# Last block of a hybrid SSD/GLA trunk: gate projections of the next-to-last head moved behind the last head's values, u in one tile per 128 features, operands of the first products split inside the block

## The chip, the core and the metric

The kernel runs on one core of one Trainium2 chip. The metric is the device time of one execution in microseconds (us). TensorE (PE) does the matmuls, VectorE (DVE) and ScalarE (ACT) the elementwise work, GpSimd (POOL) a smaller share of it, and SyncE (SP) issues most DMAs. PE and SP run in the order in which the program issues; ACT, DVE and POOL get their order from a scheduler at build time, and each then works through its own list in that order.

## What is computed

One layer of a decoder trunk on 2048 tokens (16 meta tokens ahead of them) with 1024 features, all in float32:

```python
u = rmsnorm(hres, norm_w)
proj = jnp.einsum('bld,dn->bln', u, w_in)
z, xbc, dt_raw, q, k, v, g_gla, a_lr, merge_g = split_cols(proj, IN_WIDTHS)
# y_ssd: 4 groups of a chunked state-space scan;  o: 4 heads of chunked gated linear attention (GLA)
y_gla = o.reshape(b, l, GLA_DV) * jax.nn.silu(g_gla)
branch_proj = jnp.einsum('blnc,ncd->blnd', branches, w_branch)
gates = jax.nn.sigmoid(merge_g.reshape(b, l, N_BRANCH, D_MODEL))
merged = jnp.sum(gates * branch_proj, axis=2)
return hres + jnp.einsum('bld,de->ble', merged, w_out)      # and a last rmsnorm
```

## The kernel before

**Precision.** Each float32 operand of a large matmul is split into a high part (ACT, cast to float32r) and a low part (DVE, the rest); helper `split` (L232) does the pair. `accum` (L183) then issues three matmuls per product, high by high (L185), high by low (L186) and low by high (L187). So a "projection" of 128 output features over 512 tokens is 8 x 3 = 24 matmuls of 512 columns (`proj_feat`).

**First part: four blocks of 512 tokens.** For each block `load_u` makes the normalized input u, high and low, for 8 groups of 128 features (index kt), into one tile of a pool of two (`upool`), and writes u to DRAM too (`u_left`). Then come four SSD groups (`ssd_proj`) and four GLA heads (`gla_proj`). `gla_proj` of head h projects q, k, the values v (`proj_tok`, two halves), then two gate tiles g, and starts that head's scan. A scan (`gla_scan`) is a generator with about ten steps; each `yield` of a projection runs one step of every scan that is under way, so a scan's small matmuls stand between the big projections in PE's list. The steps of a GLA scan, with their lines: score products of six levels (`level_in` L698 to L705 on DVE and ACT, `level_out` L713 on PE, merged by L717 and L720), sums for the diagonal (L783), merge and masks (L785, L788, L791), transposes of the keys (`turn_keys`, L734) and of the attention tile (L800), two state updates (`advance`: matmuls L185 to L187, DVE L809), outputs of two chunks each (L821 and L185 to L187 on PE, copy and squares L825, L828 on ACT), then the normalization (L228 DVE, L229 POOL, L832 ACT), transposes (L837) and the product with the gate (L838 DVE). In the last block the scan of the last head (3) starts right behind its values, ahead of its gates; all other heads' scans start behind their gates.

**Second part: seven matrix products** in stages (merge gates, two branches, output), each computed with seven block products p = 1..7 instead of eight per pair of tiles (`Stage`). A product is 12 matmuls of 512 columns. Its left operand comes from weight tiles (`load_a` L931, sums on POOL L940 to L943, split `prep_a` L949/L950), its right operand from u, y or the merged values in DRAM (`load_b` L919, split `prep_b` L924/L925), 4 pieces for each p. The first stage's products p = 1 and 2 take u of block 0 as right operand; p = 6 and 7 take sums that were stored earlier.

**The seam.** When the last projection is issued, the remaining scan steps run in a loop; a table `between` says what of the second part is issued ahead of each step. Before the change: loads and splits of the operands of p = 1 and p = 2, and the products p = 1 and p = 2 of the first two tile pairs (n = 0, 1) (`NEARLY = 4`). The pools of the second part lie on memory of the first: `u`, the weight tiles (`wpool`), and later the scans' tiles. A tile there can be filled only once the last reader of what lay there is done. The pools of the later operands (`bops6`, `outs`) open only behind the last scan step.

Of the kernel before, what the change touches and what calls it, by code (L numbers as in the profile page):

```python
# [14 lines left out]
P = 128  # L15
D = 1024
# [12 lines left out]
NC1 = 8  # L29
LEVELS = (64, 32, 16, 8, 4, 2)  # L30
# [10 lines left out]
def trunk_kernel(ctx: ExitStack, tc: tile.TileContext, xm, xmt, w_feat, w_tok, w_zm, w_br, w_o,  # L41
# [71 lines left out]

    inputs = ctx.enter_context(ExitStack())
    upool = inputs.enter_context(tc.tile_pool(name="upool", bufs=2))
# [85 lines left out]
    def proj_tok(key, src, u, starts, banks, width=256, per=2, sub=None):  # L201

        nq = KT // per
        opened = set()
        for q0 in range(0, nq, 2):
            if q0 == nq // 2:
                yield
            ws = [load_w(f"{key}_{q}", src[:, q * per * width:(q + 1) * per * width]) for q in (q0, q0 + 1)]  # L210
            for i, ((bk, ps), a) in enumerate(zip(banks, starts)):
                c0 = sub if sub is not None and i >= NCH else 0
                for k2 in range(2 * per):
                    kt = q0 * per + k2
                    h, lo = ws[k2 // per]
                    cs = slice(k2 % per * width + c0, (k2 % per + 1) * width)
                    accum(ps[:, c0:width], tuple(t[:, kt, a:a + P] for t in u),
                          (h[:, cs], lo[:, cs]), bk not in opened, kt == KT - 1, skip_group_check=True)
                    opened.add(bk)
# [16 lines left out]

    def load_u(b):
# [3 lines left out]
        pair = mk(upool, [P, 2, KT * (META + BLK)], F32R, "u")[:, :, :KT * tt]  # L241
        uh, ul = [pair[:, i].rearrange("p (k t) -> p k t", k=KT) for i in range(2)]

        def rows_load(r0, n, i=None):
            xt = mk(wk, [P, D], F32, "tok4", bufs=NT4) if i is None else mk(wk, [P, META + BLK], F32, "acc")[:, :BLK]
            nc.sync.dma_start(xt[:n], xm[r0:r0 + n, :] if i is None else xm[r0:r0 + n, i * BLK:(i + 1) * BLK])
            return xt
# [44 lines left out]
        if m0:  # L292
            rm = bank(pt, "pt")
            nc.tensor.matmul(rm[:, :META], rs[NCH][:META].to_broadcast([META, P]), ident[:META, :META],
                             start=True, stop=True)
            rbs = [(rm, 0, META)] + rbs
        else:
            rbc = mk(wk, [P, 3 + META + BLK], F32, "cin")[:, :BLK]
            nc.scalar.activation(rbc, rb, AF.Copy)
            rbs = [(rbc, 0, BLK)]  # L300
            yield
        for kt in range(KT):
            xk = mk(wk, [P, META + BLK], F32, "act" if m0 else "acc", bufs=NACT if m0 else 2)[:, :tt]
# [4 lines left out]
            nc.scalar.activation(uh[:, kt, :tt], xk, AF.Copy)  # L308
            nc.scalar.dma_start(u_left[b][kt], xk[:, m0:])
            nc.vector.tensor_tensor(ul[:, kt, :tt], xk, uh[:, kt, :tt].bitcast(F32), op=ALU.subtract)  # L310
            yield
        return uh, ul
# [42 lines left out]
    def new_block(b, u):  # L355
        o = Block()
        o.b, o.u = b, u
        o.m0 = META if b == 0 else 0
        o.tt = o.m0 + BLK
        o.segs_all = [(0, o.tt // 2), (o.tt // 2, o.tt // 2)] if b == 0 else [(0, BLK)]  # L360
        o.segs_real = [(o.m0, BLK)]
        o.starts = [o.m0 + c * P for c in range(NCH)]
        o.chunks = ([(0, META)] if o.m0 else []) + [(a, P) for a in o.starts]
        o.ci0 = 1 if o.m0 else 0
        o.nck = len(o.chunks)
        for nm in ("tkd", "tkc", "wde", "ecu", "dec"):
            setattr(o, nm, mk(bpool, [P, 5, NH], F32, nm, bufs=2))
# [3 lines left out]
        o.mov = lambda kt, a, n: tuple(t[:, kt, a:a + n] for t in u)  # L371
        return o


    def dt_chain(o, psd):
# [44 lines left out]
        cr = mk(wk, [P, 3 + META + BLK], F32, "cin")[:NH, :BLK]  # L420
# [39 lines left out]
    def ssd_proj(o, g):  # L460
# [16 lines left out]
        for j in range(4):  # L477
            ti = g * 4 + j
            pss = proj_feat(f"s{ti}", w_feat[T_SSD + ti], o.segs_all, o.mov)
            cin = mk(wk, [P, 3 + META + BLK], F32, "cin")  # L480
            acc = mk(wk, [P, META + BLK], F32, "acc")[:, :tt]
# [18 lines left out]
    def fetch_cb(o, g, c):  # L500
        cbs[g, c] = cb = mk(wk, [P, 4, P], F32, "cb", bufs=3)
# [113 lines left out]
    def gla_proj(o, h):  # L615
# [27 lines left out]
        yield  # L643
        for j in range(2):
# [6 lines left out]
        if not last:  # L651
            begin(gla_scan(o, h, qs, kf, (vh, vl), vm, gs))
# [208 lines left out]

    ordered = ExitStack()
    ordered.enter_context(tc.manual_schedule(engines={mybir.EngineType.PE, mybir.EngineType.SP}))
    for b in range(nblk):
        o = new_block(b, next_u[b])
        for i in range(SG + GH):
# [4 lines left out]
            if i == SG and b + 1 < nblk:  # L871
                begin(fetch_u(b + 1))
# [21 lines left out]
    bpl = {p: pool2(f"bops{p}", 4) for p in (1, 2)}  # L894
    rpl = pool2("raws", 1)
    apl = pool2("aops", 6)
    bt_raws = {"early": (rpl, "br0", 2)}
# [6 lines left out]
    class Stage:  # L904
# [16 lines left out]
        def prep_b(self, p, j):  # L921
            raw = self.braws[p, j]
            t = mk(bpl[p], [P, 2, BLK], F32R, f"b{p}")
# [13 lines left out]
        def sum_a(self, n):  # L937
            a11, a21, a22, a12 = self.araws.pop(n)
            s1, s2, s4 = [mk(rpl, [P, 4, P], F32, "as", bufs=6) for _ in range(3)]
# [13 lines left out]
        def product(self, n, p, early=False):  # L953
# [10 lines left out]
            if p in (1, 6, 5):  # L964
                sn = mk(rpl, [P, 4, P], F32, "as", bufs=6).rearrange("p k c -> p (k c)") if early else mk(opl, [P, BLK], F32, "sn", bufs=6)
                nc.scalar.activation(sn, ps, AF.Copy)  # L966
                self.snap[n, p] = sn
# [3 lines left out]


# [106 lines left out]
    NEARLY = 4  # L1079
    order[:NEARLY] = [(stages[0], n, p) for n in range(2) for p in (1, 2)]  # L1080
# [14 lines left out]
    for si, st in enumerate(stages):  # L1095
        for q in range(0 if si else 8, 28):
            p, j = PS[q // 4], q % 4
            pos = begins[si] - 12 + 0.8 * q if si else -0.99 + 0.2 * (q // 4) if q < 16 else 2 * (q // 4 - 4)
# [29 lines left out]
    st = stages[0]  # L1128

    def b_ops(p, js):  # L1130
        for j in js:
            st.load_b(p, j)
            st.prep_b(p, j)
# [20 lines left out]
    bpl.update({p: pool2(f"bops{p}", 4, side="right") for p in (6, 7, 5, 3, 4)})  # L1154
    opl, spl = pool2("outs", 1, side="right"), pool2("small", 4, side="right")
    bt_raws["all"] = opl, "br", 5

    with tc.manual_schedule(engines={mybir.EngineType.SP}):
        run(-1)
        for i, (st, n, p) in enumerate(order):  # L1160
            if i >= 2:
# [92 lines left out]
```

## Time and profile before

| | us |
|---|---|
| median of 3 runs | 2304.4 (2302.48 to 2305.96) |
| profiled execution, its own time | 2306.7 |
| its span, first to last instruction | 2304.9 |
| PE busy in the span | 2236.0 |
| DVE, ACT, POOL busy | 1546.8, 1181.4, 677.5 |
| mean granted TensorE clock | 0.989 |

The profile has a page (busy time per engine, 40 slices, the chain that ended last, the costliest groups of instructions, DMA issues), and the trace behind it answers views: stretches of time (windows) with each engine's busy time and the granted clock, waits (who waited for whom), the timeline of single instructions, and groups of instructions by line. A row of a group reads: line, engine, operation, tile written <- tiles read, shape, count | busy us, mean ns of one | idle time ahead of it and what ended it. Matmul ends are modelled and consecutive matmuls overlap, so the pace of a row of matmuls is read from start to start.

### The profile page before, as it was taken

The page shows a single profiled execution, that of the slowest core. Times are in us where ns is not written, and L with a number is a line of the kernel's source. Part 1 is how long each engine was busy: PE and PEld are TensorE (multiplying, and loading weights), DVE is VectorE, ACT ScalarE, POOL GpSimd, SP SyncE. Part 2 cuts the span into 40 slices and gives each one's busy share as a digit, 9 for nine tenths or more (in the row PEclk, how much of TensorE's full clock was granted, in tenths as well). Part 3 has the DMA queues.
Part 4 walks back from the last instruction along what each step waited for, and adds up shares of the span by engine and source line. Part 5 has one row for each costly group of instructions (what it writes and reads, how often), then busy time and mean ns, then how long its engine had stood idle before and what let it go on. Part 6 is the DMA issues. An engine that isn't in the chain of part 4 may idle for free.

```text
span 2304.9 us, 36458 instructions
## 1 busy us (share of the span) xinstructions
PE 2236.0 (97%) x12641; PEld 1954.7 (85%) x12641; DVE 1546.8 (67%) x2895; ACT 1181.4 (51%) x2726; POOL 677.5 (29%) x681
## 2 busy tenths in 40 slices
PE   7899999999999999999999999889999999999998
PEld 6899989888889888888888888778878888788786
DVE  5677676676666676666667555754588945788766
ACT  4665654465544465544455534554554545454443
POOL 3344433122222122321212100136333274324331
PEclk9999999999999999999999999999999999999999
DMA  8756776667787666887676654466677865778743
GB/s 299 236 202 221 268 262 206 220 197 241 247 263 230 210 223 216 259 262 235 200 233 209 213 159 156 138 218 207 219 246 275 312 220 204 235 268 266 245 152 121
DMA packets 301544, 518.04 MB, mean 225 GB/s; under 512 B 27696, under 2 KB 143664, under 8 KB 301360
## 3 DMA queue, kind: packets, MB, share of 16 engines
q1 hardware_dynamic: 200400, 402.84, 53.8%
q10 hardware_dynamic: 100960, 112.88, 14.0%
q8 instruction: 99, 1.62, 0.3%
q14 instruction: 85, 0.70, 0.1%
HBM read 368.42 MB, written 147.19 MB: 224 GB/s over the span
## 4 chain that ended last, share of the span: by engine, by line
PE 78%; DMA 7%; DVE 6%; ACT 4%; issue 3%; POOL 1%; SPq 0%; ACTq 0%; DVEq 0%; POOLq 0%
PE pj L185 18%; PE pj L187 18%; PE pj L186 18%; PE pt L185 3%; PE pt L187 3%; PE pt L186 3%; PE pc L574 2%; PE pc L185 2%; PE pc L186 2%; PE pc L187 2%; PE pc L713 2%; DMA br<-out_t 1%; PE pc L575 1%; PE pc L577 1%; DMA acc<-in_xmt 1%
## 5 line engine op out<-in xcount | busy, mean ns | idle before, releaser
L185 PE MATMUL pj<-u,whl 128*128 128x512 f32 (+1 forms) x1184 | 445.9, 377 | 12.3 <-ACT acc L485 6.3
L187 PE MATMUL pj<-u,whl 128*128 128x512 f32 (+1 forms) x1184 | 431.8, 365 | 0.5 <-DVE tkc L392 0.5
L186 PE MATMUL pj<-u,whl 128*128 128x512 f32 (+1 forms) x1184 | 430.9, 364 | 0.0
L185 PE MATMUL pj<-whl,u 128*128 128x256 f32 (+1 forms) x992 | 287.8, 290 | 1.8 <-ACT u L308 1.5
L187 PE MATMUL pj<-whl,u 128*128 128x256 f32 (+1 forms) x992 | 282.4, 285 | 1.5 <-DVE u L310 1.5
L186 PE MATMUL pj<-whl,u 128*128 128x256 f32 (+1 forms) x992 | 282.1, 284 | 0.0
L185 PEld LDWEIGHTS pj<-u,whl 128*128 128x128 f32 x1184 | 225.9, 191 | 50.2 <-ACT acc L485 7.6
L185 PE MATMUL pj<-b,a 128*128 128x512 f32 x640 | 254.1, 398 | 14.1 <-ACT sn L966 8.2
L187 PEld LDWEIGHTS pj<-u,whl 128*128 128x128 f32 x1184 | 225.4, 190 | 36.6 <-POOL whl L166 0.8
L186 PEld LDWEIGHTS pj<-u,whl 128*128 128x128 f32 x1184 | 226.0, 191 | 33.1
L187 PE MATMUL pj<-b,a 128*128 128x512 f32 x640 | 252.9, 395 | 0.0
L186 PE MATMUL pj<-b,a 128*128 128x512 f32 x640 | 251.7, 393 | 0.0
L80 POOL TENSOR_TENSOR wr<-wr 128x256 f32<-128x256 f32 x80 | 67.1, 839 | 432.2 <-DMA wr<-u 177.0
L185 PEld LDWEIGHTS pj<-whl,u 128*128 128x128 f32 x992 | 189.7, 191 | 3.1 <-ACT u L308 1.8
L187 PEld LDWEIGHTS pj<-whl,u 128*128 128x128 f32 x992 | 189.7, 191 | 2.2 <-DVE u L310 2.2
L186 PEld LDWEIGHTS pj<-whl,u 128*128 128x128 f32 x992 | 189.9, 191 | 0.3
L925 DVE TENSOR_TENSOR b<-br,b 128x512 fp32r<-128x512 f32 x196 | 154.8, 810 | 50.3 <-ACT b L924 49.6
L166 POOL TENSOR_TENSOR whl<-wr,whl 128x512 fp32r<-128x512 f32 (+1 forms) x100 | 133.9, 1346 | 179.8 <-ACT whl L165 127.2
L940 POOL TENSOR_TENSOR as<-ar,ar 128x512 f32<-128x512 f32 x40 | 58.2, 1455 | 417.7 <-DMA ar<-in_w_br 201.7
L489 DVE SCALAR_TENSOR_TENSOR acc<-cin,hcw,acc 128x512 f32<-128x512 f32 (+1 forms) x192 | 154.8, 806 | 27.1 <-ACT acc L485 26.2
L924 ACT ACTIVATE b<-br 128x512 fp32r<-128x512 f32 x196 | 119.2, 626 | 102.7 <-DMA br<-br_t 40.4
L950 DVE TENSOR_TENSOR a<-ar,a 128x512 fp32r<-128x512 f32 x160 | 126.8, 801 | 60.6 <-ACT a L949 59.8
(278 smaller groups left out, 5057.2 us busy)
## 6 DMA issues: line engine op xcount, KB each, us to landing
whl<-k_s SPq DMA_DIRECT2D x96, 512.0 KB, 4.3
whl<-k_g SPq DMA_DIRECT2D x96, 512.0 KB, 4.2
whl<-k_v SPq DMA_DIRECT2D x48, 512.0 KB, 3.7
whl<-k_z SPq DMA_DIRECT2D x36, 512.0 KB, 3.7
wr<-in_w_feat SPq DMA_DIRECT2D x64, 256.0 KB, 4.4
k_s<-whl SPq DMA_DIRECT2D x32, 512.0 KB, 3.6
cb<-cumd ACTq DMA_DIRECT2D x64, 256.0 KB, 5.7
y<-gg ACTq DMA_DIRECT2D x64, 256.0 KB, 4.5
```

Source lines behind the costliest of these rows:

```text
L80: nc.gpsimd.tensor_tensor(o, x, y, op=ALU.subtract)
L166: nc.gpsimd.tensor_tensor(hl[:, 1], raw, hl[:, 0].bitcast(F32), op=ALU.subtract)
L185: nc.tensor.matmul(ps, sh, mh, start=first, stop=False, **kw)
L186: nc.tensor.matmul(ps, sh, ml, start=False, stop=False, **kw)
L187: nc.tensor.matmul(ps, sl, mh, start=False, stop=last, **kw)
L489: nc.vector.scalar_tensor_tensor(acc, cin[:, k:k + tt], hcw[:, ti, k:k + 1], acc, op0=ALU.mult, op1=ALU.add)
L574: nc.tensor.matmul(py[:, h * 64:(h + 1) * 64], dm[:, h], xdt[:, h], start=True, stop=True)
L713: nc.tensor.matmul(ps[:, r * P:(r + 1) * P], kq[:, 2 * r * P:(2 * r + 1) * P], kq[:, (2 * r + 1) * P:(2 * r + 2) * P], start=True, stop=True)
L924: nc.scalar.activation(t[:, 0], raw, AF.Copy)
L925: nc.vector.tensor_tensor(t[:, 1], raw, t[:, 0].bitcast(F32), op=ALU.subtract)
L940: nc.gpsimd.tensor_tensor(s1, a21, a22, op=ALU.add)
L950: nc.vector.tensor_tensor(t[:, 1], src, t[:, 0].bitcast(F32), op=ALU.subtract)
```

## The change

Four edits go together.

- **Order.** In the last block the scans of heads 2 and 3 (`LATE_G = 2`) both start behind their own values. The two gate projections of head 2 are put aside (`late_g`) and issued behind head 3's values, ahead of head 3's own two.
- **u in tiles.** u lives in 8 tiles per block, one per 128 features: even blocks in pool `ueven`, which stays open to the end, odd blocks in `uodd`.
- **Operands of p = 1, 2.** A generator `first_b`, begun with head 0 of the last block, loads u of block 0 back from DRAM, one 128-feature tile a step, through the buffers of raw weights (`wr`), and splits it into `ueven` tiles, which the last block doesn't use.
- **The seam.** `between` is rewritten: it issues the loads of the left operands, p = 1 and 2, and now p = 6 too for n = 0, 1 (`NEARLY = 6`), with the four right operands of p = 6 loaded through one raw buffer (`br0`, 1 instead of 2). Some small tiles move to a pool (`spool`) that lies between `ueven` and `uodd`; `bops6` opens on its memory.

The diff, cut to its core:

```diff
+    ueven = ctx.enter_context(tc.tile_pool(name="ueven", bufs=KT))
-    upool = inputs.enter_context(tc.tile_pool(name="upool", bufs=2))
+    spool = inputs.enter_context(tc.tile_pool(name="spool", bufs=2))
+    uodd = inputs.enter_context(tc.tile_pool(name="uodd", bufs=KT))
...
+    def u_tile(b):
+        return mk(uodd, [P, 2, BLK], F32R, "uo") if b % 2 else mk(ueven, [P, 2, META + BLK], F32R, "ue")
...
-        last, gs = (o.b, h) == (nblk - 1, GH - 1), []
+        last, gs = o.b == nblk - 1 and h >= LATE_G, []
         if last:
-            begin(gla_scan(o, h, qs, kf, (vh, vl), vm, gs, True))
+            begin(gla_scan(o, h, qs, kf, (vh, vl), vm, gs, h == GH - 1))
...
+        if last and h < GH - 1:
+            late_g.append(gla_gates(o, h, gs))
+            return
+        for gen in late_g:
+            yield from gen
+        late_g.clear()
+        yield from gla_gates(o, h, gs)
+        if not last:
+            begin(gla_scan(o, h, qs, kf, (vh, vl), vm, gs))
...
+    def first_b():
+        loaded = []
+        for n in range(KT + 1):
+            if n < KT:
+                raw = mk(wpool, [P, 512], F32, "wr", bufs=NWR)
+                nc.sync.dma_start(raw, u_left[0][n])
+                loaded.append(raw)
+            if n:
+                t = u_tile(0)[:, :, :BLK]
+                split(t[:, 0], t[:, 1], loaded[n - 1])
+                early_b[1 + (n - 1) // 4, (n - 1) % 4] = t
+            yield
...
-            if i == SG and b + 1 < nblk:
-                begin(fetch_u(b + 1))
+            if i == SG:
+                begin(fetch_u(b + 1) if b + 1 < nblk else first_b())
...
-    bt_raws = {"early": (rpl, "br0", 2)}
+    bt_raws = {"early": (rpl, "br0", 1)}
...
     between = {
-        0: [lambda: st.load_a(0), lambda: b_ops(1, (0, 1))],
-        1: [lambda: b_ops(1, (2, 3)), lambda: st.prep_a(0, 1)],
-        2: [lambda: st.load_a(1), lambda: b_ops(2, (0, 1))],
-        3: [lambda: b_ops(2, (2, 3)), lambda: st.prep_a(0, 2)],
-        4: [lambda: st.product(0, 1, True), lambda: st.prep_a(1, 1)],
-        5: [lambda: st.sum_a(0)],
-        6: [lambda: st.product(0, 2), lambda: st.prep_a(1, 2)],
-        7: [lambda: st.sum_a(1)],
+        0: [lambda: st.load_a(0), lambda: st.load_a(1), lambda: st.load_b(6, 0)],
+        1: [],
+        2: [lambda: st.prep_a(0, 1), lambda: st.prep_a(1, 1)],
+        3: [lambda: early(0, 1), lambda: st.prep_a(0, 2)],
+        4: [lambda: st.sum_a(0), lambda: early(1, 1), lambda: st.prep_a(1, 2)],
+        5: [lambda: early(0, 2), lambda: st.prep_b(6, 0), lambda: st.load_b(6, 1)],
+        6: [lambda: early(1, 2), lambda: st.sum_a(1), lambda: st.prep_b(6, 1), lambda: st.load_b(6, 2)],
+        7: [lambda: st.prep_a(0, 6), lambda: st.prep_b(6, 2), lambda: st.load_b(6, 3)],
+        8: [lambda: st.prep_b(6, 3), lambda: early(0, 6), lambda: st.prep_a(1, 6)],
+        9: [lambda: early(1, 6)],
     }
```

More of the change, by code (lines that the diff above doesn't have):

```diff
@@ L210, in proj_tok @@
             ws = [load_w(f"{key}_{q}", src[:, q * per * width:(q + 1) * per * width]) for q in (q0, q0 + 1)]
-            for i, ((bk, ps), a) in enumerate(zip(banks, starts)):
-                c0 = sub if sub is not None and i >= NCH else 0
+            for n, ((bk, ps), a) in enumerate(zip(banks, starts)):
+                c0 = sub if sub is not None and n >= NCH else 0
                 for k2 in range(2 * per):
@@ L370, in new_block @@
         o.alr = mk(bpool, [P, 5, 48], F32, "alr")
[L371 removed]
+        o.mov = lambda kt, a, n: tuple(u[kt][:, i, a:a + n] for i in range(2))
         return o
@@ L964, in product @@
             if p in (1, 6, 5):
-                sn = mk(rpl, [P, 4, P], F32, "as", bufs=6).rearrange("p k c -> p (k c)") if early else mk(opl, [P, BLK], F32, "sn", bufs=6)
-                nc.scalar.activation(sn, ps, AF.Copy)
-                self.snap[n, p] = sn
+                if early and p == 6:
+                    return
+                self.snapshot(n, p, early)
             if p in DONE:
@@ L1078, in trunk_kernel @@
             order += [(st, n + i, p) for p in ps for i in range(2)]
-    NEARLY = 4
-    order[:NEARLY] = [(stages[0], n, p) for n in range(2) for p in (1, 2)]
+    NEARLY = 6
     AHEAD, LOAD = 5, 9
@@ L1153, in trunk_kernel @@
     first.close()
-    bpl.update({p: pool2(f"bops{p}", 4, side="right") for p in (6, 7, 5, 3, 4)})
+    bpl.update({p: pool2(f"bops{p}", 4, side="right") for p in (7, 5, 3, 4)})
     opl, spl = pool2("outs", 1, side="right"), pool2("small", 4, side="right")
     bt_raws["all"] = opl, "br", 5
+    for n in range(2):
+        st.snapshot(n, 6)
     with tc.manual_schedule(engines={mybir.EngineType.SP}):
```

65 lines of the change are left out of this document (39 added, 26 removed).

## The prediction

> **What bounds the kernel now.** I read the page first, then stretches of time, then PE's timeline where a stretch isn't full. The page's head and busy line:
>
> ```profile
> span 2304.9 us, 36458 instructions
> PE 2236.0 (97%) x12641; PEld 1954.7 (85%) x12641; DVE 1546.8 (67%) x2895; ACT 1181.4 (51%) x2726; POOL 677.5 (29%) x681
> ```
>
> PE is the bound. The change removes no matmul: set side by side, the two builds issue the same 11,908 PE instructions, 2897 on DVE, 2979 on ACT. So only PE's idle time and lost clock can change. The stretches around the seam (columns: PE, PEld, DVE, ACT, POOL busy, then PEclk):
>
> ```profile
> 1300.00:1415.00 115.00, 115.00 (x723) 103.96 (x722) 58.98 (x147) 48.93 (x127) 7.17 (x9) 1.00 0.51 159
> 1415.00:1460.00 45.00, 45.00 (x281) 40.54 (x280) 26.12 (x64) 18.29 (x49) 1.58 (x1) 1.00 0.53 169
> 1460.00:1480.00 20.00, 16.17 (x88) 13.59 (x86) 16.12 (x41) 8.56 (x21) 0.00 (x0) 1.00 0.34 118
> 1480.00:1500.00 20.00, 13.14 (x61) 11.62 (x62) 17.48 (x37) 11.49 (x29) 8.93 (x6) 0.74 0.43 137
> 1500.00:1520.00 20.00, 14.15 (x70) 11.86 (x69) 8.04 (x14) 11.12 (x27) 4.77 (x4) 0.96 0.33 115
> 1520.00:1545.00 25.00, 23.87 (x92) 18.77 (x92) 17.98 (x28) 17.91 (x32) 3.10 (x3) 0.89 0.86 289
> 1545.00:1645.00 100.00, 100.00 (x439) 82.09 (x438) 48.89 (x62) 46.91 (x82) 58.67 (x55) 1.00 0.67 220
> ```
>
> PE is full on both sides and loses time from 1472 to 1541 only. Every idle piece there, from PE's timeline (the bracket holds the idle time and what ended it):
>
> ```profile
> 1474.31 0.71 PE L713 MATMUL pc<-sq 128*128 128x128 f32 x4 [1.39 <-DVE c L720]
> 1476.15 0.70 PE L821 MATMUL pc<-s_gla,act 128*128 128x256 f32 x2 [1.13 <-DVE c L809]
> 1481.50 1.22 PE L713 MATMUL pc<-sq 128*128 128x128 f32 x4 [2.81 <-ACT junk L828]
> 1483.25 1.23 PE L713 MATMUL pc<-sq 128*128 128x128 f32 x4 [0.53 <-DVE c L720]
> 1493.46 0.41 PE L800 MATMUL pt<-cst,sq 128*128 128x128 f32 x2 [4.17 <-DVE sq L791]
> 1499.33 0.38 PE L185 MATMUL pc<-tok,kdt 128*128 128x256 f32 x1 [0.66 <-DVE c L809]
> 1519.50 1.22 PE L185 MATMUL pj<-b,a 128*128 128x512 f32 x2 [5.85 <-ACT b L924]
> 1540.30 0.51 PE L185 MATMUL pj<-b,a 128*128 128x512 f32 x1 [1.13 <-ACT sn L966]
> ```
>
> Their sum is 17.7 us. After three of them the clock stands at half for a while:
>
> ```profile
> 1480.90:1487.70 6.80, 5.67 (x20) 4.97 (x21) 6.32 (x17) 3.72 (x10) 0.00 (x0) 0.50 0.75 252
> 1494.60:1498.00 3.40, 3.40 (x16) 3.13 (x14) 3.40 (x5) 0.91 (x3) 3.40 (x3) 0.51 0.03 8
> 1518.50:1525.30 6.80, 5.80 (x14) 4.50 (x15) 3.97 (x6) 4.51 (x8) 0.00 (x0) 0.50 0.87 291
> ```
>
> Half of the 5.67 + 3.40 + 5.80 busy us is lost: 7.4. **The seam costs 17.7 + 7.4 = 25.1 us**, the ceiling of what this change can bring. What PE waits for: to 1500, head 3's scan, with head 2's in the same DVE list and only two gate projections as filler; at 1519.5, the right operands of p = 6, whose loads wait for the scan's last transposes.
>
> **Part 1, the order: about 11 us more filler.** One projection's length, from its first matmul to what follows it:
>
> ```profile
> 1458.77 0.47 PE L185 MATMUL pj<-u,whl 128*128 128x512 f32 x1
> 1464.33 0.60 PE L713 MATMUL pc<-sq 128*128 128x128 f32 x4
> 1465.47 0.61 PE L713 MATMUL pc<-sq 128*128 128x128 f32 x4
> ```
>
> 5.56 us; two are 11.1. Behind head 3's values now stand four, 22.2 us, and by the new order about 10 us of the scans' own matmuls: 32 us in which head 3's scan can reach its last level product. Does it? Before, values ended about 1457 and that product came at 1487.4, 30 us, of which DVE was busy 33.6 of the 40 us to 1500 with both scans and eight low parts of b. Now those eight are gone from here, and head 2's scan is 11 us further ahead, since it waits for values only. Adding such rows' durations along the new DVE list, each piece no earlier than the matmul it waits for, I find head 3's work ahead of the last level product done some 4 us before PE gets there. The tightest place is head 3's first level product: before, 8.4 us after the values (1465.47, no idle time); now 9.1. So PE stays full to the end of the fourth projection, and the 1.39, 1.13, 2.81 and 0.53 go. Cost if this cover fails: up to those 5.9 us.
>
> **Then the chain is bare.** Behind the fourth projection the new PE list has the last level product and the sums (1.14 us from start to start, 1464.33 to 1465.47), head 2's transposes and the key transposes (about 1.3): 2.45 us. The attention transposes (L800) wait meanwhile for this DVE list, with the same operations' rows from before:
>
> ```profile
> L785 DVE COPY_PREDICATED c<-msk,pt 128x256 f32<-128x256 uint8 x2 | 0.9, 435 | 0.0
> L788 DVE TENSOR_TENSOR sq<-c,cst 128x512 f32<-128x512 f32 x2 | 1.4, 688 | 0.0
> L791 DVE COPY_PREDICATED sq<-msk,pt 128x512 f32<-128x512 uint8 x2 | 1.4, 724 | 0.0
> L648 DVE SCALAR_TENSOR_TENSOR gg<-gg,pj 128x512 f32<-128x512 f32 x2 | 1.4, 678 | 0.0
> L838 DVE SCALAR_TENSOR_TENSOR gg<-pt,hgw,gg 128x512 f32<-128x512 f32 x4 | 3.0, 744 | 2.0 <-PE pt L837 2.0
> L950 DVE TENSOR_TENSOR a<-ar,a 128x512 fp32r<-128x512 f32 x4 | 2.8, 689 | 1.9 <-ACT a L949 1.9
> L647 ACT ACTIVATE gg<-pj 128x512 f32<-128x512 f32 x2 | 1.2, 591 | 2.5 <-PE pj L187 2.5
> ```
>
> In its order: tanh of the last gate (0.59), L648 0.68, L785 0.44, L838 0.74, L788 0.69, L838 0.74, L950 0.69, L791 0.72: 5.3, less some 0.07 overlap for each of seven, with 0.2 for the hand-overs: 5.0. **PE idles 5.0 - 2.45 = 2.5 us** (4.17 before).
>
> Behind it no product stands between state updates and outputs any more: before, p = 1 stood there (22 matmuls from 1500.13 to 1505.14 in the timeline); now both p = 1 products come after the last outputs. So PE sees: the attention's low parts behind two low parts of a, two L950 (0.7); state updates (0.3); and, ahead of the last outputs, the copy and squares of the first, whose bank they take:
>
> ```profile
> 1500.40 0.60 ACT L825 ACTIVATE ot<-pc 128x512 f32<-128x512 f32 x1 [4.64 <-PE pc L187]
> 1501.67 0.19 ACT L828 ACTIVATION_READ_ACCUMULATOR junk<-pc 128x1 f32 x1
> ```
>
> 1.46 us, 0.4 of it beside the state matmuls: 1.1. **Sum 2.1 us**; between nothing (all hidden) and 4.9, if it is as uncovered as two chains of 2.45.
>
> **Part 2, clock.** Does 2.5 us of idle time halve the clock?
>
> ```profile
> 1999.90 0.79 PE L185 MATMUL pj<-b,a 128*128 128x512 f32 x1 [2.12 <-ACT sn L966]
> 1999.80:2003.10 3.30, 3.20 (x8) 2.53 (x9) 2.39 (x4) 2.61 (x6) 0.00 (x0) 0.50 0.19 70
> ```
>
> 2.12 us did, for 3.3 us; 1.13 at 1540.30 came into a full-speed stretch. I take one such window over a tail that is partly waiting anyway: **1.5 us** (ends: 0 and, for a 6.8 us window, 3.4). The Trainium skill (TensorE: Matmul & The Clock Gate, section "What's actually happening") has the clock fall after at least one idle window of about 3.4 us; by that rule 2.5 us would cost no clock, and the sum would be 1.5 us lower. The 2.12 us row speaks against it.
>
> **Part 3, operands of p = 1, 2, 6.** Rows of before for a split and for the normalization (cast, low part, POOL's power, ACT's scaling):
>
> ```profile
> L924 ACT ACTIVATE b<-br 128x512 fp32r<-128x512 f32 x11 | 6.4, 620 | 1.3 <-DMA br<-u 1.3
> L925 DVE TENSOR_TENSOR b<-br,b 128x512 fp32r<-128x512 f32 x8 | 5.8, 741 | 1.0 <-ACT b L924 1.0
> L229 POOL TENSOR_TENSOR rstd<-rstd,mhalf 128x4 f32<-128x4 f32 x2 | 2.4, 1196 | 50.1 <-DVE rstd L228 50.1
> L832 ACT ACTIVATE ot<-ot,rstd 128x256 f32<-128x256 f32 x12 | 5.1, 496 | 1.1 <-POOL rstd L229 1.1
> ```
>
> Eight loads, eight casts (0.62 each) and eight low parts (0.74) move from the seam into heads 0 and 1 of the last block: there DVE is busy 59 of 115 us and ACT 49, so 5.9 and 5.0 more are hidden by PE's 115 of 115; uncovered they would cost that. On SP they stand between weight loads; PE's waits from 1290 to 1472 are none, so those loads have room. The p = 6 operands now load on memory that is free early, so **the 5.85 us go, and their 2.9 of clock**. But they come one at a time through one buffer, and ACT's list has the second piece's cast ahead of the copy of the last outputs. A 256 KB load alone, and in a crowd:
>
> ```profile
> 1490.90 2.75 DMA br<-u
> 1515.01 5.87 DMA br<-gate_t
> ```
>
> That load starts when the first piece's low part is done, about when the second state update is. The normalization behind it is 1.46 (copy, squares), 1.2 on POOL, four scalings that take 5.1 / 12 = 0.43 each; the two p = 1 products that hide all this last 24 x 0.233 = 5.6. With 2.75 the transposes L837 wait 0, with 5.87 about 1.9: **0.9 us**. The other three pieces have 18 us (p = 1, transposes, p = 2 and part of p = 6) for three rounds of load and split, 2.75 to 5.87 plus 1.36 each; I take nothing, 4 at the far end. What is late next, p = 7, loads after the transposes with 11 us of p = 2 and 6 as cover: nothing. The 1.13 at a snapshot (L966) stays: **1.1**.
>
> **Part 4, u in tiles.** Blocks 0 to 3 up to head 0 of the last block keep order and waits on every engine, and so does the time after the first stage. The first left operands can load once the last projection has read its first feature tiles, not all of u; as the product that needs them comes over 12 us later, that is worth nothing here.
>
> **The sum.** Left at the seam: 2.5 + 2.1 + 1.5 + 0.9 + 1.1 = 8.1 us, of 25.1. Gain 17.0. The profiled span 2304.9 becomes 2287.9 (its own time, 2306.7, 2289.7); the runs' median is 2304.4, 0.5 below the span: **2287.4**.
>
> **Rivals.**
> - *The clock stays full* (the Trainium skill's rule above) and the load is fast: 8.1 - 1.5 - 0.9 leaves 5.7, gain 19.4, 2285.0. For it: at 1540.30 nothing happened; against it: 2.12 us was enough elsewhere.
> - *ACT's list holds the tail*: the second piece lands late (5.87), the last outputs' copy waits, the transposes with it, and the idle time halves the clock again: 1.9 - 0.9 + 3.4 + some late p = 6, gain 12 to 13, 2292.
> - *The waiting moves on*: the scan's chain is as slow as before (4.17 again, 4.9 between the states, both at half clock) and p = 6 waits its 4 us. Left: 4.2 + 4.9 + 3.4 + 4 = 16.5 with the snapshot's; gain 8.6, 2296. Against it: before, DVE had two low parts of b in the 4.6 us from the sums to L800, and the clock was just back from half.
> - *Nothing*: first-stage operands arrive no earlier, PE reaches them sooner and waits: within 5 us of now. Against it: in 1520 to 1545 PE was held 1.1 us while 20 pieces came.
> - *Slower*: place, SP's list in heads 0 and 1. A raw load waits for its buffer until the split three loads back is done; weight loads stand behind it. If each of eight were held past the weights' lead, one projection's 5.6 us or so, and by 3 us more, PE would lose 8 x 3 = 24 against 17 gained: 2311. It decides from 2.1 us a piece. Against it: the split awaited is three projections, 16 us, old, and blocks 1 and 2 carry more such loads with no idle time.
>
> **How the numbers follow.** Forecast 2287.4: 0.47. Full clock 2285.0: 0.15. ACT held 2292: 0.15. Moves on 2296: 0.11. Nothing: 0.05. Slower: 0.07. Range 2283 to 2296: from the ceiling less 4 us of left idle time to the fourth case, which it holds half. 0.2% is 4.6 us, about what a measurement here can tell from none. Faster (under 2299.8) 0.88, same 0.05, slower 0.07.
>
> **What would show it.** In PE's waits of the new profile: at the seam no L713 row, no L924 row of 5.8; an L800 row of about 2.5; rows of 1 or less at L185 and L821; an L837 row up to 2. Half clock in one window. A wait for `whl` in heads 0 and 1 would be the slower case; a wait for b6 of over 3 us would break part 3; idle time ahead of the fourth gate projection's end, part 1.

## The result: 11.8 us faster, 6 us short of the forecast

The changed kernel takes **2293.55 us** (median of five runs, 2291.95 to 2295.66); the kernel before, in runs beside it, 2305.37 (2302.48 to 2306.14). The ratio is 0.9951, 95% interval 0.9937 to 0.9966: faster by half a per cent, clear of the noise, and 6.1 us above the 2287.4 of the forecast. The profiled span fell by 12.9 us, from 2304.9 to 2292.0, where 17.0 was forecast. Head and busy line of the page after:

```profile
span 2292.0 us, 36448 instructions
PE 2232.7 (97%) x12641; PEld 1944.7 (85%) x12641; DVE 1549.2 (68%) x2895; ACT 1180.1 (51%) x2726; POOL 683.8 (30%) x681
```

The counts of matmuls and of DVE's and ACT's instructions are those of before, PE is 3.3 us less busy, and the rest of the gain is idle time. Lines have moved: L800 is now L819 (attention transposes), L713 L732 (level products), L828 L847 (squares), L821 L840 (outputs), L837/L838 L856/L857 (output transposes, gate products), L924/L925 L958/L959 and L949/L950 L983/L984 (splits of b and a), L966 L1010 (snapshot: the copy of a product's PSUM bank to SBUF, ahead of the next product that adds to the bank), L940 to L943 L974 to L977 (POOL's sums). The same stretches as before (busy time of PE, PEld, DVE, ACT, POOL, then PEclk):

```profile
1300.00:1415.00 115.00, 115.00 (x727) 104.23 (x727) 66.69 (x160) 54.56 (x140) 7.24 (x9) 1.00 0.55 176
1415.00:1460.00 45.00, 43.28 (x272) 38.78 (x271) 32.06 (x84) 19.86 (x54) 1.01 (x1) 1.00 0.44 145
1460.00:1480.00 20.00, 18.08 (x100) 15.48 (x99) 10.86 (x29) 8.42 (x23) 1.01 (x1) 1.00 0.27 91
1480.00:1500.00 20.00, 15.76 (x85) 12.52 (x84) 11.01 (x21) 9.89 (x25) 2.27 (x2) 1.00 0.50 159
1500.00:1520.00 20.00, 19.08 (x84) 14.43 (x83) 16.58 (x19) 12.13 (x23) 15.01 (x10) 1.00 0.75 235
1520.00:1545.00 25.00, 23.62 (x99) 18.29 (x99) 19.78 (x23) 13.65 (x25) 17.24 (x16) 1.00 0.80 258
1545.00:1645.00 100.00, 100.00 (x437) 81.75 (x436) 51.45 (x66) 49.22 (x86) 50.07 (x45) 1.00 0.64 212
```

The clock column is full in every row (0.74, 0.96 and 0.89 before), and 1480 to 1500 has 15.8 us of PE instead of 13.1. But 1415 to 1460, full before, now lacks 1.7 us, and 1500 to 1545 still lacks 2.3. PE's pieces with idle time ahead of them (in brackets), of 0.3 us or more:

```profile
1429.82 0.71 PE L732 MATMUL pc<-sq 128*128 128x128 f32 x4 [0.54 <-DVE c L739]
1439.76 1.16 PE L732 MATMUL pc<-sq 128*128 128x128 f32 x8 [1.19 <-ACT junk L847]
...
1466.26 1.16 PE L732 MATMUL pc<-sq 128*128 128x128 f32 x8 [1.39 <-ACT junk L847]
1475.45 0.71 PE L732 MATMUL pc<-sq 128*128 128x128 f32 x4 [0.53 <-DVE c L739]
1483.53 0.66 PE L856 MATMUL pt<-cst,ot 128*128 128x128 f32 x4 [0.33 <-DVE c L804]
1486.76 0.41 PE L819 MATMUL pt<-cst,sq 128*128 128x128 f32 x2 [1.93 <-DVE sq L810]
1488.77 0.39 PE L189 MATMUL pc<-tok,atp 128*128 128x256 f32 x1 [0.36 <-ACT atp L237]
1489.62 0.38 PE L191 MATMUL pc<-tok,atp 128*128 128x256 f32 x1 [0.34 <-DVE atp L238]
1490.34 0.70 PE L840 MATMUL pc<-c,act 128*128 128x256 f32 x2 [0.34 <-DVE c L828]
1493.05 0.70 PE L840 MATMUL pc<-c,act 128*128 128x256 f32 x2 [0.95 <-ACT junk L847]
...
1519.36 0.74 PE L189 MATMUL pj<-b,a 128*128 128x512 f32 x2 [0.78 <-ACT b L958]
1520.76 0.51 PE L190 MATMUL pj<-b,a 128*128 128x512 f32 x1 [0.66 <-DVE b L959]
1526.91 0.50 PE L189 MATMUL pj<-b,a 128*128 128x512 f32 x1 [0.51 <-ACT sn L1010]
```

With pieces under 0.3 us the sum is 10.2 us, against 17.7. The 5.85 ahead of p = 6 is gone and the 4.17 at the attention transposes is 1.93, as forecast. What was not forecast: 3.65 us at level products while projections still run (first four rows; the first two are head 2's level products, in front of and between the halves of head 3's values, the other two head 3's, between gate projections), and the waits of p = 5 at 1519 and 1520.

**A measure that noise spares.** Executions of one kernel differ by several us in places far from the seam: in the profiles of this case one group of waits in the first 160 us (L492) takes from 5.3 to 8.1 us, those at the snapshots behind 2000 us from 3.8 to 7.3. So I compare the profiles by one stretch of PE's own list, from the last state product ahead of the last block's head 2 (1384.8 after) to a matmul of the first stage behind all that differs (1582.4 after), cut at the last head's sums and at its last output. us:

| kernel | to the sums | sums to last output | from there on | whole stretch |
|---|---|---|---|---|
| before | 102.0 | 18.7 (one product p = 1 of 5.1 within) | 88.5 | 209.2 |
| changed | 97.0 | 12.8 | 87.8 | 197.6 |
| changed, second profile | 97.1 | 12.4 | 87.5 | 196.9 |

11.6 of the 12.9 us arise here. What follows uses the times for the verdicts and this stretch for the parts.

### The profile page after: what moved, and what is told of

Read it like the earlier page. It is cut to its first block, busy times and chain, and to the rows that moved or that the text cites. A ratio compares the mean times of both kernels' runs of the same rounds, so it can differ in the third digit from the quotient of the medians.

```text
span 2292.0 us, 36448 instructions
## 1 busy us (share of the span) xinstructions
PE 2232.7 (97%) x12641; PEld 1944.7 (85%) x12641; DVE 1549.2 (68%) x2895; ACT 1180.1 (51%) x2726; POOL 683.8 (30%) x681
## 5 line engine op out<-in xcount | busy, mean ns | idle before, releaser
L189 PE MATMUL pj<-ue,whl 128*128 128x264 f32 (+1 forms) x672 | 238.8, 355 | 12.3 <-ACT acc L492 6.3
L191 PE MATMUL pj<-ue,whl 128*128 128x264 f32 (+1 forms) x672 | 232.3, 346 | 0.6 <-DVE tkc L399 0.6
L190 PE MATMUL pj<-ue,whl 128*128 128x264 f32 (+1 forms) x672 | 231.3, 344 | 0.0
L189 PE MATMUL pj<-uo,whl 128*128 128x512 f32 x512 | 206.6, 404 | 0.0
L191 PE MATMUL pj<-uo,whl 128*128 128x512 f32 x512 | 200.1, 391 | 0.0
L190 PE MATMUL pj<-uo,whl 128*128 128x512 f32 x512 | 199.4, 389 | 0.0
L189 PE MATMUL pj<-b,a 128*128 128x512 f32 x480 | 189.4, 396 | 6.6 <-ACT sn L1010 5.8
L191 PE MATMUL pj<-b,a 128*128 128x512 f32 x480 | 188.6, 393 | 0.0
L190 PE MATMUL pj<-b,a 128*128 128x512 f32 x480 | 187.8, 391 | 0.7 <-DVE b L959 0.7
L974 POOL TENSOR_TENSOR as<-ar,ar 128x512 f32<-128x512 f32 x40 | 59.1, 1476 | 396.3 <-DMA ar<-in_w_br 114.2
L984 DVE TENSOR_TENSOR a<-ar,a 128x512 fp32r<-128x512 f32 x160 | 125.5, 793 | 57.0 <-ACT a L983 55.3
L959 DVE TENSOR_TENSOR b<-br,b 128x512 fp32r<-128x512 f32 x140 | 120.5, 877 | 52.6 <-ACT b L958 50.7
L189 PEld LDWEIGHTS pj<-ue,whl 128*128 128x128 f32 x672 | 128.9, 192 | 29.9 <-ACT acc L492 7.4
L189 PE MATMUL pj<-whl,ue 128*128 128x256 f32 (+1 forms) x496 | 144.1, 291 | 2.1 <-ACT ue L315 2.1
L189 PE MATMUL pj<-whl,uo 128*128 128x256 f32 (+1 forms) x496 | 143.3, 289 | 0.6 <-DMA whl<-k_zm 0.6
L191 PEld LDWEIGHTS pj<-ue,whl 128*128 128x128 f32 x672 | 128.9, 192 | 15.8 <-POOL whl L170 0.9
L191 PE MATMUL pj<-whl,ue 128*128 128x256 f32 (+1 forms) x496 | 140.6, 284 | 1.4 <-DVE ue L317 1.4
L190 PEld LDWEIGHTS pj<-ue,whl 128*128 128x128 f32 x672 | 129.1, 192 | 14.8
L191 PE MATMUL pj<-whl,uo 128*128 128x256 f32 (+1 forms) x496 | 140.8, 284 | 0.0
```

What stands on the lines that cost most here:

```text
L189: nc.tensor.matmul(ps, sh, mh, start=first, stop=False, **kw)
L190: nc.tensor.matmul(ps, sh, ml, start=False, stop=False, **kw)
L191: nc.tensor.matmul(ps, sl, mh, start=False, stop=last, **kw)
L959: nc.vector.tensor_tensor(t[:, 1], raw, t[:, 0].bitcast(F32), op=ALU.subtract)
L974: nc.gpsimd.tensor_tensor(s1, a21, a22, op=ALU.add)
L984: nc.vector.tensor_tensor(t[:, 1], src, t[:, 0].bitcast(F32), op=ALU.subtract)
```

## Experiments

**Each part alone.** The kernel before with only the gates' order changed:

```diff
-        last, gs = (o.b, h) == (nblk - 1, GH - 1), []
+        last, gs = o.b == nblk - 1 and h >= LATE_G, []
...
+        if last and h < GH - 1:
+            late_g.append(gla_gates(o, h, gs))
+            return
```

> The kernel before with the order of the last block's gates alone: head 2's two gate projections run behind head 3's values; operands of the first stage, u and pools as before. Theory A (both parts earn, each at its own place): the idle time up to the attention transposes falls from 13.2 us (1.39, 1.13, 2.81, 0.53, 4.17, 0.66 and 2.5 between) to 6 or so, the 5.85 us wait for the right operands of p = 6 stays and halves the clock behind it: gain 3 to 6 us, 2299 to 2302. Rival B (the gain is the operands' alone): gain under 1 us, about 2304.5. Rival C (all of it is the order): gain 10 or more, 2295 or less.

Measured: 2300.19 us, ratio to before 0.9978 (0.9967 to 0.9988); stretch 206.1, so 3.1 less than before: theory A's size. Up to the last head's sums it takes 97.1, as in the changed kernel. The rest is spoilt; three of its waits and a stretch:

```profile
1492.71 0.41 PE L813 MATMUL pt<-cst,sq 128*128 128x128 f32 x2 [1.93 <-DVE sq L804]
...
1519.42 0.73 PE L186 MATMUL pj<-b,a 128*128 128x512 f32 x2 [0.92 <-ACT b L937]
1522.40 0.79 PE L187 MATMUL pj<-b,a 128*128 128x512 f32 x1 [2.25 <-DVE b L938]
```

```profile
1500.00:1520.00 20.00, 17.98 (x75) 14.46 (x73) 12.40 (x17) 12.37 (x30) 11.70 (x9) 0.81 0.59 191
```

The attention transposes wait the same 1.93 as in the changed kernel (4.17 before), so the order alone is enough for that gain. p = 6 still waits, 3.2 us and not the 5.85 that theory A kept: its loads still begin only behind the last output transposes (1513.06), but PE reaches it 5.4 us after that, with two products p = 2 in between. And the clock is lost: 0.81 over these 20 us.

The changed kernel with the order of before:

```diff
-LATE_G = 2
+LATE_G = 3
```

> The changed kernel with LATE_G = 3: operands, u and pools as changed, the last block's projections in the order of before (head 2's gates ahead of its scan and of head 3). Theory A: the 5.85 us wait and its half clock go (8.7 us), the new waits at p = 7 and p = 5 (1.7 us and some slower matmuls) come; the 1.39, 1.13, 2.81, 0.53 and 4.17 ahead of the transposes stay within 1 us: gain 6 to 8, 2297 to 2299. Rival B (operands alone earn everything): gain 11 to 12, 2293 to 2294. Rival C (all of it is the order): gain under 2.

Measured: 2296.99 us, ratio 0.9970 (0.9959 to 0.9982); stretch 202.0, 7.2 less than before: theory A again. With 3.1 that makes 10.3 of 11.6; neither part earns it all. One point of theory A fails: the 4.17 ahead of the attention transposes doesn't stay, 1.20 is left there and 1.77 at the sums in front. What the old order leaves at the seam:

```profile
1474.43 0.71 PE L732 MATMUL pc<-sq 128*128 128x128 f32 x4 [1.37 <-DVE c L739]
1476.28 1.22 PE L840 MATMUL pc<-s_gla,act 128*128 128x256 f32 x2 [1.13 <-DVE c L828]
1482.07 1.16 PE L732 MATMUL pc<-sq 128*128 128x128 f32 x8 [1.73 <-ACT junk L847]
```

**u in tiles alone**: the kernel before with the new pools and `u_tile`, nothing else.

```diff
-        pair = mk(upool, [P, 2, KT * (META + BLK)], F32R, "u")[:, :, :KT * tt]
+        u = []
...
+            u.append(u_tile(b)[:, :, :tt])
```

> The kernel before with u in tiles per 128 features, two pools of them, and nothing else of the change. Prediction's step (u in tiles is worth nothing by itself): within 1 us of before in the stretch from 1384 to 1582, within 0.2% in time. Rival (blocks gain because a tile of u comes free before the block's last projection): faster by 2 us or more, in the blocks ahead of the seam.

Measured: 2301.69 us beside 2303.02 for before, ratio 0.9993 (0.9984 to 1.0003): nothing, as forecast. Its stretch is 206.7, 2.5 shorter, missing the 1 us I gave it; 1.8 of that is clock, 0.83 against 0.74 in the 20 us from 1480.

**Why level products wait (3.65 us).** The releaser of the two longest waits is the last of ACT's squares (L847), which read the PSUM bank; pool `pc` has two. Edit, on all heads:

```diff
-                nc.scalar.activation(jk, po[:, i], AF.Square, accum_out=ssq[:, c:c + 1])
+                nc.scalar.activation(jk, ot[:, c], AF.Square, accum_out=ssq[:, c:c + 1])
```

> The changed kernel with one edit: the squares behind an output copy read the copy (ot, in SBUF) and not the PSUM bank, so a bank is held for the copy (0.60 us) and not for copy and squares (1.47). Theory A1 (in the seam PE waits for the two banks of pool pc): the 1.19, the 1.39 and the 0.95 us in front of a level product or an output each lose up to 0.87; with what DVE then holds, gain 1.5 to 2.6 over the changed kernel, about 2291.5. Rival A2 (those products wait for the scan's DVE list, and the bank is only released last by chance): the same gaps stand, now ended by DVE, and the time stays within 0.5 us of 2293.5.

Measured: 2299.96 us, ratio to before 0.9975 (0.9962 to 0.9988), the changed kernel's 0.9951 (0.9937 to 0.9966): no gain, rather a loss, against both theories. The stretch is 198.6, 1.0 longer.

```profile
1446.63 0.71 PE L732 MATMUL pc<-sq 128*128 128x128 f32 x4 [1.28 <-DVE s_gla L828]
...
1472.85 0.71 PE L732 MATMUL pc<-sq 128*128 128x128 f32 x4 [0.84 <-DVE c L739]
1481.31 0.71 PE L732 MATMUL pc<-sq 128*128 128x128 f32 x4 [0.24 <-ACT ot L844]
...
1522.57 0.50 PE L190 MATMUL pt<-b,a 128*128 128x512 f32 x1 [1.30 <-DVE b L959]
1527.63 0.50 PE L190 MATMUL pj<-b,a 128*128 128x512 f32 x1 [1.71 <-DVE b L959]
1534.45 0.50 PE L189 MATMUL pj<-b,a 128*128 128x512 f32 x1 [1.50 <-ACT sn L1010]
```

Three things to see. The 1.19 only moves on, as 1.28, to the next level product, and is now ended by DVE's state update (L828): there DVE's list holds PE (A2). The 1.39, 0.53 and the 0.95 at the outputs fall to 0.84, 0.24 and 0.04: that part was the bank (A1). So of the 3.65 only 0.8 is the squares' hold on a bank. And what was won by 1500, 2.0 us by the sums of the waits, is back at p = 7, p = 5 and the snapshot. The rest of the slower time comes from the blocks ahead: waits in the SSD scans (L592, L611), 4.0 us in all, where the changed kernel's two profiles have 0 and 0.2. The edit touches every head and so ACT's list there; that this is the reason wasn't shown.

**What holds p = 7 and p = 5.** p = 7 waits 0.10 and p = 5 1.44. SP issues the loads of p = 5's right operands (`br<-gate_t`) behind those of the left operands of pair 2, which wait for buffers:

```profile
1506.08 5.68 SPq L965 DMA_DIRECT2D ar<-in_w_feat  x4
1513.34 2.64 SPq L953 DMA_DIRECT2D br<-gate_t  x4
```

One number puts p = 5's loads and splits a slot (the place of one product in the program's order) ahead:

```diff
-            pos = begins[si] - 12 + 0.8 * q if si else {3: -0.5, 4: 5.5, 5: 6.5, 6: 8.5}[q // 4]
+            pos = begins[si] - 12 + 0.8 * q if si else {3: -0.5, 4: 4.6, 5: 6.5, 6: 8.5}[q // 4]
```

> The changed kernel with one number changed: the right operands of p = 5 are loaded and split one slot earlier, so that their loads stand on the SP list ahead of the left operands of pair 2 and not behind them. Theory A3 (SP's order makes the operands late: those loads were issued at 1513.3 to 1515.7 behind loads that waited for POOL's sums): the waits at p = 7 and p = 5 (0.10, 0.78, 0.66, 0.19) fall to 0.5 in all and the matmuls there go back to some 0.23 us each: gain 1.5 to 3 over the changed kernel, about 2291.5. Rival A4 (the low parts are late because DVE works at 1.77 us an operation there beside POOL's sums, and not 0.68): the loads land earlier, the waits stay over 1.2 us, gain under 0.7.

Measured: 2296.72 us, ratio 0.9963 (0.9951 to 0.9976); stretch 198.0, no gain, but 6.8 us of it are at half clock (0.83 in the 20 us from 1480, where the changed kernel has 1.00); from the last output on it takes 87.3, the changed kernel 87.8 and 87.5. The waits of the first products p = 7 and p = 5 are gone, and others have taken their place:

```profile
1526.11 0.51 PE L189 MATMUL pj<-b,a 128*128 128x512 f32 x1 [1.73 <-ACT sn L1010]
1529.63 0.50 PE L190 MATMUL pj<-b,a 128*128 128x512 f32 x1 [0.72 <-DVE b L959]
```

Neither theory foresaw that: the waits did fall, and the snapshot of p = 5, for which p = 3 waits, now stands in ACT's list behind casts of b that wait for their loads. (The expectation of the next run calls it p = 6's bank; by the order of the products it is p = 5's.) There remained A4, DVE's pace beside POOL. DVE, then POOL, in the changed kernel:

```profile
1506.91 0.69 DVE L1026 TENSOR_TENSOR as<-as,pc 128x512 f32<-128x512 f32 x1 [0.40 <-PE pc L191]
...
1513.84 3.48 DVE L959 TENSOR_TENSOR b<-br,b 128x512 fp32r<-128x512 f32 x2
1517.24 1.77 DVE L984 TENSOR_TENSOR a<-as,a 128x512 fp32r<-128x512 f32 x1
1519.34 3.66 DVE L959 TENSOR_TENSOR b<-br,b 128x512 fp32r<-128x512 f32 x3 [0.33 <-ACT b L958]
1522.92 0.68 DVE L984 TENSOR_TENSOR a<-ar,a 128x512 fp32r<-128x512 f32 x1
```

```profile
1506.03 1.63 POOL L975 TENSOR_TENSOR as<-as,ar 128x512 f32<-128x512 f32 x1
...
1513.48 1.60 POOL L977 TENSOR_TENSOR as<-ar,as 128x512 f32<-128x512 f32 x1 [4.56 <-DMA g<-as]
1515.35 1.43 POOL L974 TENSOR_TENSOR as<-ar,ar 128x512 f32<-128x512 f32 x1 [0.27 <-DMA ar<-in_w_feat]
1516.85 1.61 POOL L975 TENSOR_TENSOR as<-as,ar 128x512 f32<-128x512 f32 x1
```

Two low parts take 3.48 us beside POOL's sums; alone one takes 0.68. Their ends follow POOL's: L984 (1517.24 + 1.77 = 1519.01) ends 0.55 us after L975 (1516.85 + 1.61 = 1518.46). The operation of 1506.91, which reads one operand from PSUM, takes 0.69 beside a POOL sum. So the sums were moved two slots later for pairs 2 and 3, and their loads with them, behind those of p = 5:

```diff
-            at(i - LOAD + (n % 2), lambda st=st, n=n: load_sum_a(st, n))
+            at(i - (LOAD - 2 if i < 20 else LOAD) + (n % 2), lambda st=st, n=n: load_sum_a(st, n))
```

> The changed kernel with the left operands of pairs 2 and 3 of the first stage loaded and summed two slots later, so that POOL's sums and the DMA waits behind them stand after the right operands of p = 5, not ahead of them; nothing else moves on purpose. The run before this showed that b5 loaded one slot earlier takes the waits at p = 7 away (1.5 us) and hands 1.2 of it to the copy of p = 6's bank, so no gain. Theory A4 (DVE's 1.77 us operations beside POOL's sums make the low parts late): the low parts at p = 7 and p = 5 take some 0.7 us again, waits of both and the snapshot under 1.2 us in all, gain 1 to 2 in the stretch from 1384 to 1582. Rival A5 (the casts and copies in ACT's list are the limit, and what is cut at one operand comes back at the next): the sum of waits behind 1500 stays at 2.2 or more, and the stretch within 0.5 us of the changed kernel's.

Measured: 2291.93 us, ratio 0.9943 (0.9924 to 0.9962); stretch 195.2, 2.4 less than the changed kernel, a little more than A4 said, and this with 3.4 us at half clock in it. DVE and a stretch of it; the same stretch of the changed kernel behind:

```profile
1513.30 1.72 DVE L984 TENSOR_TENSOR a<-as,a 128x512 fp32r<-128x512 f32 x1
1514.94 1.88 DVE L959 TENSOR_TENSOR b<-br,b 128x512 fp32r<-128x512 f32 x3
```

```profile
1510.00:1520.00 10.00, 10.00 (x44) 7.92 (x44) 9.18 (x14) 8.07 (x16) 1.29 (x1) 1.00 0.74 241
```

```profile
1510.00:1520.00 10.00, 9.08 (x37) 6.22 (x35) 9.52 (x11) 6.61 (x13) 6.18 (x4) 1.00 0.92 302
```

Three low parts now take 1.88 together (the 1.72 stands beside the one POOL sum left there), DVE does 14 operations and PE 44 matmuls where it did 11 and 37. Not only idle time goes: the matmuls of the second p = 7 and the first p = 5 had also started further apart (290 and 287 ns without the waits, 250 and 229 here). The move changes SP's order and POOL's time together; that the operations are short again is POOL's part, and how much the earlier loads add isn't told apart.

**Both causes at once.** Late sums, and the squares of the last block's last two heads from SBUF:

```diff
-                nc.scalar.activation(jk, po[:, i], AF.Square, accum_out=ssq[:, c:c + 1])
+                nc.scalar.activation(jk, (ot[:, c] if o.b == nblk - 1 and h >= LATE_G else po[:, i]), AF.Square, accum_out=ssq[:, c:c + 1])
```

> The same, and the squares of the last block's last two heads read the copy in SBUF and not the PSUM bank. With that edit on all heads the waits up to 1500 fell by 2.4 us, and 2.5 us of waiting came back at p = 7, p = 5 and the copy of p = 6's bank, as PE got there sooner. Theory A4: with the operands in time the 2.4 stay: stretch 3 to 4.5 us shorter than the changed kernel's, time about 2290. Rival A5 (a floor behind 1500 set by the operands' own chain, whenever PE gets there): the waits come back again, gain under 1.5.

Measured: 2291.53 us, ratio 0.9939 (0.9922 to 0.9956); stretch 194.4, 3.3 less than the changed kernel, as A4 said. By the waits' sums up to 1500 the edit on all heads had won 2.0 us, not the 2.4 of this expectation. A floor behind 1500 (A5) would have eaten the gain; only 0.81 us of waiting is left there. Half clock takes part of it, 0.17 of 20 us or 6.8 us at a half:

```profile
1480.00:1500.00 20.00, 17.71 (x82) 14.19 (x81) 11.77 (x23) 11.18 (x26) 4.84 (x4) 0.83 0.44 138
```

**The 1.93 us ahead of the attention transposes, longer.** One DVE copy of the scores onto themselves, then three:

```diff
+        for _ in range(1 if last else 0):
+            nc.vector.tensor_copy(att, att)
```

> The changed kernel with one more DVE copy of the attention scores onto themselves, in the last head of each block, between the last select and the transposes that wait for it: the idle time of 1.93 us there becomes about 2.6. It tells what idle time halves the clock at this place. By the row of 2.12 us idle and 3.3 us at half clock elsewhere, the clock is at a half in the windows behind, and the stretch grows by 0.7 + 1.5 or more. Rival (no half clock below some 3.4 us): the stretch grows by 0.7 at most and the clock stays full.

> The same with three more copies: idle about 4.0 us. Both theories have the clock at a half behind it; its length tells what the seam costs when the wait is not shortened: by one window of 3.4 us, 1.7 us beside the 2.1 of the copies, by two, 3.4.

The wait of the first, from PE's timeline:

```profile
1487.44 0.66 PE L821 MATMUL pt<-cst,sq 128*128 128x128 f32 x2 [4.92 <-DVE sq L815]
```

In the kernel with one copy (lines from 815 on moved by two) the wait is 4.92 and not 2.6: the one copy, 0.43 us itself, came behind low parts of a and of the attention on DVE's list, one of which waits for a DMA. So it says nothing on 2.6 us. The stretch is 201.3, 3.7 more than the changed kernel's for 3.0 more of waiting, with 6.8 us at half clock behind it; the time of that one run is 2293.85. Three copies: wait 6.45 (4.5 more), 10.2 us at half clock, stretch 201.5 (3.9 more), 2297.11. So a longer wait at this place costs about its length or less, half clock included, as other waits of the stretch shrink meanwhile: from 8.3 us in all to 7.7 and 6.7.

**The same wait, shorter.** On top of late sums and squares, in the step where both scans end, head 3 goes first:

```diff
-        for gen in list(running):
+        for gen in running[::-1] if flip else list(running):
...
-            step()
+            step(k == 0)
```

> The kernel with late sums and squares from SBUF, and in the one step where both scans end, head 3's key and attention transposes, and first state update, are emitted ahead of head 2's output transposes, so that the two gate products of head 2 (0.74 us each) and one low part (0.68) no longer stand on the DVE list between the sums and the last select. Theory (the attention transposes wait for these three): the select ends some 1.4 us earlier; 0.9 us of transposes leave the time ahead of it and fill the waits between states and outputs (1.0 us in the changed kernel). Stretch from 1384 to 1582 0.5 to 1.4 us shorter than in the run with late sums and squares, time 2290 to 2291. Rival (the chain is ACT's and PE's hand-overs, not these three operations): stretch the same within 0.3 or longer, as the gate products come back in front of the state updates.

> The changed kernel once more, beside the other kernels of this call. If an idle time of 1.93 us halves the clock or not by its place against a fixed raster (after five kernels with the same 1.93 us wait, three showed no half clock behind it and two showed 3.4 and 6.8 us of it), this profile may show either at the same wait; if the kernel's own order decides, it shows none again. Time within 2 us of 2293.5; stretch from 1384 to 1582 197.6, or 1 to 3 more with a half clock.

Measured on one chip: 2287.77 us (2286.91 to 2288.4), the changed kernel 2294.36 (2290.29 to 2295.15), before 2303.02; ratios to before 0.9938 (0.9925 to 0.9950) and 0.9961 (0.9947 to 0.9975). The changed kernel is where it was, its second profile shows the 1.93 us wait and again no half clock behind it. **The turned version beats both**, by 6.6 us and 15.3. Its waits from 1480 on:

```profile
1486.27 0.41 PE L819 MATMUL pt<-cst,sq 128*128 128x128 f32 x2 [2.37 <-DVE sq L810]
1491.91 0.70 PE L840 MATMUL pc<-c,act 128*128 128x256 f32 x2 [0.28 <-DVE c L828]
...
1522.92 0.50 PE L189 MATMUL pj<-b,a 128*128 128x512 f32 x1 [1.06 <-ACT sn L1010]
```

The attention transposes come 1.2 us earlier than with late sums and squares, counted from the stretch's start. The wait itself is longer, 2.37, because 0.9 us of transposes that filled it now stand behind; there they fill the small waits of states and outputs. From the sums to the last output it takes 10.2 us, 12.8 in the changed kernel and 11.5 in the one with squares from SBUF alone, which had no half clock either: 1.3 us for the turn, inside the forecast. The stretch, 191.7, is 2.6 less than with late sums and squares, but the clock was at half there and is full here, so that difference says less.

## Why the prediction was right in sign and 6 us too low

The best kernel's stretch less its 6.5 us of idle time is 185.25, with the clock full: a yardstick for these matmuls. Against it, before loses 209.2 - 185.25 = 24.0, the changed kernel 12.4: 10.2 idle and 2.2 of matmuls that start further apart. The latter come with the waits: at the wait of 0.66 in p = 5 the matmul ahead of it and the one behind it take 0.40 and 0.34 us (waiting left out), where 0.23 from start to start is usual, so this wait costs some 0.28 us beyond its bracket. The prediction had 25.1 and 8.1. Step by step:

- **Ceiling 25.1**: 24.0. What is left for the half clock is 209.2 - 185.25 - 17.7 = 6.3, not 7.4; that part of the halved busy time would have been waited for anyway is likely, not shown.
- **Part 1, "PE stays full to the end of the fourth projection": failed**, 3.65 us. The new order puts filler there, but a level product that comes right behind a state update or an output of the other scan on PE's list still waits, for that scan's copy and squares in one of two banks (0.8 to 1.0 of it, by the runs with squares from SBUF) or for operations on DVE's list (the rest, by its releasers alone). The prediction weighed head 3's first and last level product; 1.92 us came at head 3's products in between, and 1.73 at head 2's, which it didn't look at. This is the largest miss.
- **Attention transposes 2.5**: 1.93, and 0.33 at head 2's transposes. Right, and DVE's list in between is the forecast one, operation by operation.
- **States and outputs 2.1**: 0.36 + 0.34 + 0.34 + 0.95 = 2.0. Right.
- **Clock 1.5**: 0 in both profiles of the changed kernel, inside the stated ends; other kernels with the same wait did lose clock (below).
- **Part 3**: the 5.85 and its clock went, as said. Head 3's output transposes (L856) wait 0, not 0.9; the snapshot 0.5, not 1.1. **"What is late next, p = 7: nothing" failed**: p = 7 waits 0.10, but p = 5, for which the sum has no term, 1.44, and p = 4 0.19. With them come the 2.2 of matmuls further apart, 1.4 of it in the second p = 7 and the first p = 5. POOL's sums beside DVE's low parts and SP's order make these operands late.
- **Part 4, nothing**: right.

The sum: 8.1 + 3.65 + 1.7 + 2.2 - 1.5 - 0.9 - 0.6 - 0.3 of small ones make 12.4. The rest of the 12.9 us between the profiles, 1.3, lies away from the seam.

Of the rivals, *slower* did not come: 1300 to 1415 is full in the profile after. *ACT's list holds the tail* gave nearly the time, 2292, by another cause, so by luck: the transposes do not wait. *The waiting moves on* is what happened in kind, at p = 5 instead of p = 6, and smaller; its slow scan chain did not come. *The clock stays full* is true of the changed kernel, but its 2285 had the rest right, which it wasn't.

**The clock stays open.** Behind a wait of 1.92 or 1.93 us at the same transposes it was full in three profiles (the changed kernel's two, squares on all heads) and at half in four (order alone, p = 5 first, late sums, sums and squares); behind 2.37 it was full. So the length of the idle time alone doesn't decide at this size, and to put 1.5 us on it, between 0 and 3.4, was the most that the trace gave. The Trainium skill (TensorE: Matmul & The Clock Gate, section "What's actually happening") has windows of about 3.4 us that run freely; the half clock here lasted 3.4, 6.8, 10.2 or 13.6 us, which agrees. Its condition, at least one idle window, doesn't fit a half clock behind 1.92 us here. Which position against such a raster decides wasn't shown.

## What to carry to other kernels

Filler on the critical engine covers a wait only if the order of its list leaves room between the piece that frees a buffer and the piece that needs it: walk each bank and each list, not only the last chain. When a hole is closed, the engine arrives sooner at everything behind; ask of each later operand which lists it passes, and move work without a deadline (here POOL's sums for the pair after next) out of that time. Measure such a change by a stretch of the bound engine's list: here the time of single executions moved by 5 us for reasons far from the change.

## What the runs showed of the hardware

A DVE low part, with both operands in SBUF, took 0.68 us alone and up to 1.79 where it started while a POOL sum ran (changed kernel, 1500 to 1600). Its end then came 0.55 us (0.54 to 0.59) after the sum's, however early it had started, as if it waited for POOL and then ran. A DVE sum with one operand in PSUM took 0.67 to 0.69 beside POOL. I had not priced this at all. The Trainium skill (SBUF — State Buffer, section "Who interferes with whom") says that a DVE instruction with two SBUF inputs contends with a POOL instruction that reads SBUF and that one with a single SBUF input, outside the two-port modes, doesn't; the trace agrees on both.
